# Later ScalarE slots behind VectorE, wider state-space parameter products and shorter recurrence bursts in a two-block float32 kernel

## The chip, the core and the metric

The kernel runs on one core of one Trainium2 chip. The metric is the time of one execution on the device in microseconds, as the median of three. The core's engines run side by side, each through its own queue in order: TensorE (PE, with its weight loads PEld) multiplies, VectorE (DVE) and ScalarE (ACT) work element by element, GpSimd (POOL) and SyncE (SP) issue DMAs here, and ScalarE issues some too. An engine that waits for another holds up all that stands behind it in its queue.

## What is computed

Two transformer blocks on 256 positions (272 in the second) of width 2048, batch 1, in float32. The lines that matter here:

```python
# block 1: token mixing, then a feed-forward with a causal width-3 convolution
p = h @ w_in + b_in                     # u, v, q, k, v_att, z_pool and three gates
merged = (g_sgu * (y_sgu @ w_sgu_out) + g_moba * (y_moba @ w_moba_out)
          + g_pool * (y_pool @ w_pool_out))          # g = sigmoid(gates)
z = h @ w_up
z = w_conv[0] * z2 + w_conv[1] * z1 + w_conv[2] * z + b_conv
gate, val = jnp.split(z, 2, axis=-1)
y = (jax.nn.gelu(gate) * val) @ w_down
...
# block 2: latent attention beside a state-space scan, both gated
y = s5_scan(u, ...)                     # x_t = a * x_(t-1) + B u_t,  y_t = Re(C x_t) + d u_t
y = jax.nn.gelu(y)
ssm_out = (y @ w_glu_val[l]) * jax.nn.sigmoid(y @ w_glu_gate[l])
mixed = jax.nn.sigmoid(g[:, :, 0]) * attn_out + jax.nn.sigmoid(g[:, :, 1]) * ssm_out
h = h + mixed @ w_out[l]
m = rms_norm_2(h, norm_ffn[l])
h = h + (jax.nn.silu(m @ w_ffn_gate[l]) * (m @ w_ffn_up[l])) @ w_ffn_down[l]
```

## The kernel before

**Weights.** Every weight tile of 1 MB is loaded by SyncE (`load_to`) into one of nine `raw` buffers and split into two parts in two half pieces (`split_piece`): ScalarE copies the high part `wh` (L245), VectorE subtracts to get the low part `wl` (L246, in the same nine buffers). Activations are split in the same way. A product is then a pair of matmuls (`mm2`): `wh` against both activation parts at once, 512 columns (L366), and `wl` against the high part, 256 columns (L368). A unit of 16 such pairs fills one of four PSUM tiles `pm`; `join` empties it with a ScalarE copy (L372) and a VectorE addition (L373).

**The order.** It is written out by hand, by generators. The program is a list of units. `run_units` writes a unit's matmuls, and then four *slots*: in each it advances every open evacuation generator by one step (`advance`), oldest first, and then writes one weight half piece for a unit ahead. A `yield` in an evacuation thus means: the next step comes one slot later. After the four slots, one step of the side work (the attention of the block, `pump`) and `bgn` steps of the background work are written: 1.25 a unit for `s5_prep` (the parameters of the state-space scan, during feed-forward 1) and 1 a unit for `s5` (the scan itself, during the input products of block 2 and attention). The modulation rows (`ada`, L547, 128x2048) take the place of a weight piece now and then.

**The stages**, by the profile's time in us: input products of block 1 to 300; gates and the three branches (`block1_in`: `gate`, `branch`) 300 to 640; feed-forward 1 (`ffn1`, four blocks of 22 up-projection units and 12 down-projection units) 690 to 1420; input products of block 2 (`block2_in`) 1500 to 1860, of which the last 32 units are gates (`gfn`); latent attention (`attention2`, with `mla` as side work) from 1860 in units of only four pairs (or triples); state-space gating, output projection (`block2_out`); feed-forward 2 (`ffn2`) 2330 to the end.

**The evacuations that change.** `gate` and `gfn`: join, next slot a tanh on ScalarE (L810, L1416). `branch`: join, product (L834), sum (L838), and for the last branch the activation split (L403, L404). `upfn` in `ffn1`: join, the convolution's first tap on ScalarE (L1234), two taps on VectorE (L1236, L1238), then a Gelu on ScalarE (L1243) for a gate, or a product (L1248) and the activation split (L390, L392) for a value. `ffn2` has the same shape without the convolution.

**The state-space scan.** `s5_prep` works in eight groups. A group multiplies its B by three powers and its C by four powers of the complex decay, one power at a time with six VectorE instructions of 128x128 (`cmul` L1591 to L1596, and L1695 to L1700) and a `yield` behind each power. `s5` runs the recurrence over 66 chunk steps of eight 128x32 instructions on VectorE (L1784 to L1791), with a `yield` after every fourth, and then the output part: per group three reloads `MT` from DRAM (L1801), twelve small matmuls (L1820 to L1822), per two groups a Gelu (L1826), stores `yS` (L1830) and at the end reloads `yD` (L1837) with their splits (L1846, L1847).

Temporaries come from 36 pages of 128x544 (`pg`) and 20 half pages (`hp`).

Of the kernel before, what the change touches and what calls it, by code (L numbers as in the profile page):

```python
# [12 lines left out]
OP = mybir.AluOpType  # L13
# [148 lines left out]
class Kernel:  # L162
    def __init__(self, ctx, tc, ins, out):
        self.tc, self.nc, self.ins, self.out = tc, tc.nc, ins, out
        pool = lambda n, b, **k: ctx.enter_context(tc.tile_pool(name=n, bufs=b, **k))
        self.cp = pool("cp", 1)
        self.wp = pool("wp", 4)
        self.pp = pool("pp", 1)
        self.ps = pool("ps", 4, space=bass.MemoryType.PSUM)
        self.dp = pool("dp", 1, space=bass.MemoryType.DRAM)  # L170
        ctx.enter_context(tc.manual_schedule())
        self.NB = 3
        self.NPG, self.NHP, self.NRAW, self.NW = 36, 20, 9, 4
        self.uid = 0
        self.items, self.raw, self.wt = [], {}, {}
        self.loaded = self.split = self.half = 0
        self.units = []
        self.evq, self.side, self.bg, self.bgn, self.bga = [], [], [], 0, 0.0
        self.sda = 0.0
        self.nstep = 0  # L180
# [76 lines left out]
    def ahead_to(self, last, n):  # L257
# [4 lines left out]
        return last  # L262


    def unit(self, items, fn, ahead=3, pump=1, stages=4, bg=True, flush=False):
# [522 lines left out]
    def block1_in(self):  # L788
# [17 lines left out]
        def gate(store, j, bidx):  # L806
            def fn(p):
                o = self.join(p)
                yield
                nc.scalar.activation(o, o, AF.Tanh, scale=0.5, bias=self.hb[:, bidx:bidx + 1])  # L810
                store[j] = o
            return fn
# [4 lines left out]
        def branch(name, ysrc, n4, tg, place):  # L817
            it = self.add_item(ins[name][n4])
            for jj in range(4):
# [8 lines left out]
                def ev(n, p):  # L828
# [10 lines left out]
                    if place == 2:  # L839
                        yield  # L840
                        xt = self.act_tile()
                        self.split_act(xt, self.mg[n], 0.5)
                        self.X1[n] = xt
# [377 lines left out]
    def ffn1(self):  # L1221
# [5 lines left out]
        def upfn(i):  # L1227
# [3 lines left out]
            def g(p):  # L1231
                z, c = self.join(p), self.hp()[:, :T]
                yield
                nc.scalar.activation(c, z, AF.Identity, scale=self.v("w_conv2", idx), bias=self.v("b_conv", idx))  # L1234
# [6 lines left out]
                if not val:  # L1241
                    yield
                    nc.scalar.activation(c, c, AF.Gelu_apprx_tanh)  # L1243
                    gates[j] = c
                else:
                    while j not in gates:
                        yield
                    nc.vector.tensor_tensor(c, gates.pop(j), c, op=OP.mult)  # L1248
                    yield
                    xt = self.act_tile()  # L1250
# [77 lines left out]
    def block2_in(self):  # L1328
# [83 lines left out]
        def gfn(j):  # L1412
            def g(p):
                o = self.join(p)
                yield
                nc.scalar.activation(o, o, AF.Tanh, scale=0.5)  # L1416
                yield
                nc.scalar.dma_start(self.gd[:, j], o)
            return g
# [178 lines left out]
    def s5_prep(self):  # L1598
# [7 lines left out]
        lr, li, ls = (sv[:, i * 32:(i + 1) * 32] for i in range(3))  # L1606
        w = [wk[:, i * 32:(i + 1) * 32] for i in range(17)]
        yield
# [23 lines left out]
        tt(apr[:, 0], mag, cs, op=OP.mult)  # L1632
        tt(api[:, 0], mag, sn, op=OP.mult)
        tmp = (w[7], w[8])
        for l in range(1, 4):
# [22 lines left out]
        tt(ci, ci, den, op=OP.mult)  # L1658
        yield

        def bc(x):
            return x[:, :, None].to_broadcast([128, 4, 32])

        def v4(x):
# [5 lines left out]
        for g in range(8):  # L1670
# [7 lines left out]
            sc = self.pg(n="s5c")  # L1678
            u1, u2, B0, B1 = (v4(sc[:, i * 128:(i + 1) * 128]) for i in range(4))
            nci = v4(self.hp(n="s5n")[:, :128])  # L1680
            self.cmul(B0, B1, br, bi, bc(cr[:, tl]), bc(ci[:, tl]), (u1, u2))
            ts(nci, c_i, -1.0, None, op0=OP.mult)
# [3 lines left out]
            yield  # L1686
            for j in range(3):
                pr, pi = bc(apr[:, 2 - j, tl]), bc(api[:, 2 - j, tl])
                self.cmul(BA[0][:, :, j], BA[1][:, :, j], B0, B1, pr, pi, (u1, u2))
                yield  # L1690
            yield
            CA = [v44(self.pg(n="CA")) for _ in range(2)]
            for l in range(4):
                pr, pi = bc(apr[:, l, tl]), bc(api[:, l, tl])
                tt(u1, c_r, pr, op=OP.mult)  # L1695
                tt(u2, c_i, pi, op=OP.mult)
                tt(CA[0][:, :, l], u1, u2, op=OP.subtract)
                tt(u1, nci, pr, op=OP.mult)
                tt(u2, c_r, pi, op=OP.mult)
                tt(CA[1][:, :, l], u1, u2, op=OP.subtract)  # L1700
                yield

# [29 lines left out]
    def s5(self):  # L1732
# [49 lines left out]
        for c in range(1, 67):  # L1782
# [8 lines left out]
            tt(ci, ci, tm[3], op=OP.add)  # L1791
            if c % 4 == 3:
                yield
# [58 lines left out]
    def block2_out(self):  # L1852
# [10 lines left out]
        for i in range(8):  # L1863
            ig = self.add_item(ins["w_gg"][i])
            iv = self.add_item(ins["w_gv"][i])
            for it, kind in ((ig, 0), (iv, 1)):
                for jj in range(2):
# [10 lines left out]
                    def ev(n, p, kind):  # L1878
                        if kind == 0:
                            o = self.join(p)  # L1880
                            yield
                            nc.scalar.activation(o, o, AF.Tanh, scale=0.5)
# [101 lines left out]
    def ffn2(self):  # L1984
# [4 lines left out]
        def upfn(i):  # L1989
            j, val = divmod(i, 2)  # L1990

            def g(p):
                v = self.join(p)
                yield
                if not val:
                    nc.scalar.activation(v, v, AF.Silu)
                    gates[j] = v
                else:
# [4 lines left out]
                    v = None  # L2003
                    yield
                    xt = self.act_tile()
# [67 lines left out]
```

## Time and profile before

| | |
|---|---|
| median of 3 runs | 3058.28 us (3053.97 to 3065.57) |
| the profiled execution's own time | 3066.25 us |
| its span, first to last instruction | 3064.5 us |
| TensorE busy | 2935.0 us (96%) |
| VectorE busy | 2136.2 us (70%) |
| ScalarE busy | 1477.6 us (48%) |
| GpSimd busy | 56.9 us (2%), 109 instructions |
| mean granted TensorE clock | 0.981 |

A row of the profile names the line of the kernel, the engine, what is written and read, and a duration. L366 is line 366. Idle time stands in brackets or behind a bar, with the work that ended it. "PEclk" is the granted share of TensorE's full clock; 0.50 is the lower of its two levels.

### The profile page before, as it was taken

To read this page: it belongs to the slowest core of one execution; us is meant where nothing else is said; L and a number is where in the kernel's file an instruction comes from. 1 tells how busy PE (TensorE), PEld (TensorE's weight loads), DVE (VectorE), ACT (ScalarE), POOL (GpSimd) and SP (SyncE) were. 2 spreads that over 40 slices of the span, in tenths; PEclk is the share of its full clock that TensorE was granted. 3 is DMA by queue.
4 is the path that set the end of the run, shared out by engine and by line. 5 is a ranking of instruction groups with operands and counts; after the bars stand their busy time and mean duration, and the time that the engine had idled before them with its cause. 6 is when DMAs were issued, how large, how long until landed. Compare 5 with 4: busy or idle time off the path is not lost.

```text
span 3064.5 us, 41672 instructions
## 1 busy us (share of the span) xinstructions
PE 2935.0 (96%) x16204; PEld 2508.0 (82%) x16204; DVE 2136.2 (70%) x3789; ACT 1477.6 (48%) x2443; POOL 56.9 (2%) x109
## 2 busy tenths in 40 slices
PE   6999989889999999999899899999999999999998
PEld 4998878778788787887799787778888888888887
DVE  7889989877878888777546956656655545555555
ACT  5445445456554545455444344445445434444343
POOL 0000000000000000000000000000000000000000
PEclk9999999999999999999899998999999999999999
DMA  9977768774466676655465574235664555555554
GB/s 363 351 290 276 265 249 342 263 275 161 162 233 244 210 270 235 217 192 189 153 227 185 176 256 156 98 133 208 222 217 164 178 196 191 189 187 187 193 188 129
DMA packets 127224, 660.39 MB, mean 215 GB/s; under 512 B 23009, under 2 KB 36065, under 8 KB 57393
## 3 DMA queue, kind: packets, MB, share of 16 engines
q1 hardware_dynamic: 86258, 603.30, 54.6%
q10 hardware_dynamic: 34464, 35.47, 3.7%
q0 software_dynamic: 6304, 18.95, 1.7%
q8 instruction: 128, 2.10, 0.3%
q14 instruction: 70, 0.57, 0.1%
HBM read 632.42 MB, written 25.23 MB: 215 GB/s over the span
## 4 chain that ended last, share of the span: by engine, by line
PE 65%; DVE 22%; ACT 9%; issue 3%; DMA 1%; ACTq 0%; SPq 0%; DVEq 0%
PE pm L366 19%; PE pm L368 10%; DVE wl L246 7%; PE pm L384 7%; PE pm L386 7%; PE pm L385 7%; ACT wh L245 5%; DVE raw L547 3%; PE pm L352 3%; PE pm L353 3%; PE pm L354 3%; DVE hp L1238 1%; DVE hp L373 1%; DVE hp L1236 1%; ACT hp L1234 1%
## 5 line engine op out<-in xcount | busy, mean ns | idle before, releaser
L366 PE MATMUL pm<-act,wh 128*128 128x512 f32 x4704 | 1674.8, 399 | 28.5 <-DVE hp L373 18.7
L246 DVE TENSOR_TENSOR wl<-raw,wh 128x1024 fp32r<-128x1024 f32 (+1 forms) x972 | 1144.4, 1197 | 302.6 <-ACT wh L245 289.1
L368 PE MATMUL pm<-act,wl 128*128 128x256 f32 x4704 | 1328.3, 282 | 24.2 <-DVE wl L246 24.1
L366 PEld LDWEIGHTS pm<-act,wh 128*128 128x128 f32 x4704 | 890.3, 189 | 243.5 <-DVE hp L373 23.0
L245 ACT ACTIVATE wh<-raw 128x1024 fp32r<-128x1024 f32 (+1 forms) x972 | 968.8, 1030 | 242.5 <-PE pm L385 114.4
L368 PEld LDWEIGHTS pm<-act,wl 128*128 128x128 f32 x4704 | 892.7, 190 | 35.3 <-DVE wl L246 33.8
L384 PE MATMUL pm<-wh,act 128*128 128x512 f32 (+1 forms) x1072 | 430.4, 401 | 15.3 <-ACT act L738 6.1
L386 PE MATMUL pm<-wl,act 128*128 128x512 f32 (+1 forms) x1072 | 425.9, 397 | 0.7 <-DVE wl L246 0.7
L385 PE MATMUL pm<-wh,act 128*128 128x512 f32 (+1 forms) x1072 | 424.9, 396 | 0.5 <-DVE act L740 0.5
L373 DVE TENSOR_TENSOR hp<-hp,pm 128x256 f32<-128x256 f32 x336 | 140.1, 417 | 301.3 <-ACT hp L372 301.2
L372 ACT ACTIVATE hp<-pm 128x256 f32<-128x256 f32 x336 | 125.5, 377 | 425.4 <-PE pm L368 406.0
L384 PEld LDWEIGHTS pm<-wh,act 128*128 128x128 f32 (+1 forms) x1072 | 202.4, 189 | 68.3 <-ACT wh L245 7.2
L386 PEld LDWEIGHTS pm<-wl,act 128*128 128x128 f32 (+1 forms) x1072 | 202.3, 189 | 51.8 <-DVE wl L246 3.5
L385 PEld LDWEIGHTS pm<-wh,act 128*128 128x128 f32 (+1 forms) x1072 | 202.8, 189 | 50.3 <-DVE act L740 1.5
L352 PE MATMUL pm<-act,wh 128*128 128x256 f32 (+1 forms) x768 | 224.0, 292 | 8.4 <-DVE qk L373 8.2
L354 PE MATMUL pm<-act,wl 128*128 128x256 f32 (+1 forms) x768 | 221.5, 288 | 1.3 <-DVE wl L246 1.3
L353 PE MATMUL pm<-act,wh 128*128 128x256 f32 (+1 forms) x768 | 222.0, 289 | 0.3 <-DVE act L740 0.3
L547 DVE SCALAR_TENSOR_TENSOR raw<-raw,cond 128x2048 f32<-128x2048 f32 x96 | 219.0, 2285 | 4.5 <-DMA raw<-w_ada 4.4
L352 PEld LDWEIGHTS pm<-act,wh 128*128 128x128 f32 x768 | 148.3, 193 | 10.7 <-DVE qk L373 9.3
L353 PEld LDWEIGHTS pm<-act,wh 128*128 128x128 f32 x768 | 148.6, 193 | 0.8 <-DVE act L740 0.7
L354 PEld LDWEIGHTS pm<-act,wl 128*128 128x128 f32 x768 | 147.5, 192 | 1.7 <-DVE wl L246 1.7
L390 ACT ACTIVATE act<-hp 128x256 fp32r<-128x256 f32 x88 | 36.8, 418 | 138.3 <-DVE hp L1248 107.4
(329 smaller groups left out, 1771.1 us busy)
## 6 DMA issues: line engine op xcount, KB each, us to landing
raw<-w_ada SPq DMA_DIRECT2D x96, 1024.0 KB, 6.1
raw<-w_up SPq DMA_DIRECT2D x88, 1024.0 KB, 4.8
raw<-w_ff SPq DMA_DIRECT2D x88, 1024.0 KB, 4.8
raw<-w_in SPq DMA_DIRECT2D x81, 1024.0 KB, 5.0
raw<-w_st SPq DMA_DIRECT2D x37, 1024.0 KB, 6.3
raw<-w_out SPq DMA_DIRECT2D x32, 1024.0 KB, 5.7
raw<-w_down SPq DMA_DIRECT2D x32, 1024.0 KB, 5.1
raw<-w_fd SPq DMA_DIRECT2D x32, 1024.0 KB, 4.9
```

Source lines behind the costliest of these rows:

```text
L245: nc.scalar.activation(vh[:, ks], r[:, ks], AF.Copy)
L246: nc.vector.tensor_tensor(vl[:, ks], r[:, ks], vh[:, ks], op=OP.subtract)
L352: nc.tensor.matmul(o, wh[:, kw, c], x[:, 0, sl], start=start, stop=False, skip_group_check=True)
L353: nc.tensor.matmul(o, wh[:, kw, c], x[:, 1, sl], start=False, stop=False, skip_group_check=True)
L354: nc.tensor.matmul(o, wl[:, kw, c], x[:, 0, sl], start=False, stop=stop, skip_group_check=True)
L366: nc.tensor.matmul(p.rearrange("p (a t) -> p a t", a=2), wh[:, kw, c], x, start=start, stop=False, skip_group_check=True)
L368: nc.tensor.matmul(p[:, T:], wl[:, kw, c], x[:, 0], start=False, stop=stop, skip_group_check=True)
L373: self.nc.vector.tensor_tensor(o, o, p[:, :T], op=OP.add)
L384: nc.tensor.matmul(o, x[:, 0, tok], wh[:, kw], start=start, stop=False, skip_group_check=True)
L385: nc.tensor.matmul(o, x[:, 1, tok], wh[:, kw], start=False, stop=False, skip_group_check=True)
L386: nc.tensor.matmul(o, x[:, 0, tok], wl[:, kw], start=False, stop=stop, skip_group_check=True)
L547: self.nc.vector.scalar_tensor_tensor(o, o, 0.5, self.cond, op0=OP.mult, op1=OP.mult, accum_out=self.m(seg, n))
```

## The change

`later(n)` is a generator of n empty steps. Where an evacuation had one `yield` between a VectorE step and a ScalarE step that needs it, there are now two or three. The parameters of the state-space scan are multiplied for all three powers of B, or all four of C, in one instruction of 128x384 or 128x512, with repeated operands; a group goes from 18 steps of background work to 14, and the reversed powers are copied once in front. The recurrence yields after every second chunk step. The software DMA's scratch shrinks from the default to 4096 bytes of a partition, and the space goes to two more pages and seven more half pages. Computed values are the same.

```diff
@@ -170,7 +170,7 @@
-        self.NPG, self.NHP, self.NRAW, self.NW = 36, 20, 9, 4
+        self.NPG, self.NHP, self.NRAW, self.NW = 38, 27, 9, 4
@@ -261,6 +261,12 @@
+    @staticmethod
+    def later(n):
+
+        for _ in range(n):
+            yield
...
@@ -806,7 +812,7 @@
                 o = self.join(p)
-                yield
+                yield from self.later(3)
                 nc.scalar.activation(o, o, AF.Tanh, scale=0.5, bias=self.hb[:, bidx:bidx + 1])
@@ -837,7 +843,7 @@
                     if place == 2:
-                        yield
+                        yield from self.later(2)
                         xt = self.act_tile()
@@ -1230,7 +1236,7 @@
                 z, c = self.join(p), self.hp()[:, :T]
-                yield
+                yield from self.later(2)
                 nc.scalar.activation(c, z, AF.Identity, scale=self.v("w_conv2", idx), bias=self.v("b_conv", idx))
@@ -1239,14 +1245,14 @@
                 if not val:
-                    yield
+                    yield from self.later(2)
                     nc.scalar.activation(c, c, AF.Gelu_apprx_tanh)
...
                     nc.vector.tensor_tensor(c, gates.pop(j), c, op=OP.mult)
-                    yield
+                    yield from self.later(2)
                     xt = self.act_tile()
@@ -1412,7 +1418,7 @@
                 o = self.join(p)
-                yield
+                yield from self.later(3)
                 nc.scalar.activation(o, o, AF.Tanh, scale=0.5)
...
@@ -1657,9 +1665,19 @@
+        for j in range(3):
+            nc.vector.tensor_copy(rev[:, 0, j], apr[:, 2 - j])
+            nc.vector.tensor_copy(rev[:, 1, j], api[:, 2 - j])
+        yield
...
+        def bc4(x):
+            return x[:, :, :, None].to_broadcast([128, x.shape[1], 4, 32])
+
+        def rp(x, n):
+            return x[:, None].to_broadcast([128, n, 4, 32])
@@ -1676,29 +1694,41 @@
...
-            for j in range(3):
-                pr, pi = bc(apr[:, 2 - j, tl]), bc(api[:, 2 - j, tl])
-                self.cmul(BA[0][:, :, j], BA[1][:, :, j], B0, B1, pr, pi, (u1, u2))
-                yield
...
+            u1, u2 = wide(t1, 3), wide(t2, 3)
+            o0, o1 = (BA[i].rearrange("p t j c -> p j t c")[:, :3] for i in range(2))
+            pr, pi = bc4(rev[:, 0, :, tl]), bc4(rev[:, 1, :, tl])
+            tt(u1, rp(B0, 3), pr, op=OP.mult)
+            tt(u2, rp(B1, 3), pi, op=OP.mult)
+            tt(o0, u1, u2, op=OP.subtract)
+            yield
+            tt(u1, rp(B0, 3), pi, op=OP.mult)
+            tt(u2, rp(B1, 3), pr, op=OP.mult)
+            tt(o1, u1, u2, op=OP.add)
+            yield
...
-            for l in range(4):
-                pr, pi = bc(apr[:, l, tl]), bc(api[:, l, tl])
-                tt(u1, c_r, pr, op=OP.mult)
-                tt(u2, c_i, pi, op=OP.mult)
-                tt(CA[0][:, :, l], u1, u2, op=OP.subtract)
-                tt(u1, nci, pr, op=OP.mult)
-                tt(u2, c_r, pi, op=OP.mult)
-                tt(CA[1][:, :, l], u1, u2, op=OP.subtract)
-                yield
+            u1, u2 = wide(t1, 4), wide(t2, 4)
+            o0, o1 = (CA[i].rearrange("p t l c -> p l t c") for i in range(2))
+            pr, pi = bc4(apr[:, :, tl]), bc4(api[:, :, tl])
+            tt(u1, rp(c_r, 4), pr, op=OP.mult)
+            tt(u2, rp(c_i, 4), pi, op=OP.mult)
+            tt(o0, u1, u2, op=OP.subtract)
+            yield
...
@@ -1789,7 +1819,7 @@
             tt(ci, ci, tm[3], op=OP.add)
-            if c % 4 == 3:
+            if c % 2:
                 yield
@@ -1878,7 +1908,7 @@
                             o = self.join(p)
-                            yield
+                            yield from self.later(2)
                             nc.scalar.activation(o, o, AF.Tanh, scale=0.5)
@@ -1991,7 +2021,7 @@
                 v = self.join(p)
-                yield
+                yield from self.later(2 if not val else 1)
...
@@ -2001,7 +2031,7 @@
                     v = None
-                    yield
+                    yield from self.later(2)
                     xt = self.act_tile()
@@ -2060,7 +2090,7 @@
-    nc = bacc.Bacc("TRN2", target_bir_lowering=False, num_devices=1)
+    nc = bacc.Bacc("TRN2", target_bir_lowering=False, num_devices=1, dynamic_dma_scratch_size=4096)
```

In feed-forward 1, ScalarE's queue between two joins. Before:

```order
L372 ACTIVATE hp_8558<-pm_8525 128x256
L245 ACTIVATE wh_8564<-raw_8437 128x1024
L1234 ACTIVATE hp_8561<-hp_8558,vecs 128x256
L245 ACTIVATE wh_8564<-raw_8437 128x1024
L390 ACTIVATE act_8574<-hp_8561 128x256
L372 ACTIVATE hp_8616<-pm_8582 128x256
```

After, at the same kind of place (line numbers are the changed kernel's: L378 is the join, L1240 the convolution's tap, L1249 the Gelu, L396 the split):

```order
L378 ACTIVATE hp_8539<-pm_8506 128x256
L245 ACTIVATE wh_8545<-raw_8434 128x1024
L1249 ACTIVATE hp_8487<-hp_8487 128x256
L245 ACTIVATE wh_8545<-raw_8434 128x1024
L1240 ACTIVATE hp_8542<-hp_8539,vecs 128x256
L1755 ACTIVATE BT_8557<-pd_8329 128x512
L1755 ACTIVATE BT_8560<-pd_8330 128x512
L378 ACTIVATE hp_8596<-pm_8563 128x256
L396 ACTIVATE act_8603<-hp_8542 128x256
```

The tap on the tile just joined has moved behind both weight copies, and the Gelu or the split has moved into the next unit, behind that unit's join.

In the gate stage of block 1, ScalarE's queue for one gate unit. Before:

```order
L372 ACTIVATE hp_3184<-pm_3151 128x256
L810 ACTIVATE hp_3184<-hp_3184,hb 128x256
L245 ACTIVATE wh_3193<-raw_3077 128x1024 x2
L400 ACTIVATE act_3199<-hp_3136 128x256
L950 ACTIVATE hp_3204<-pd_3202,vecs 128x256
```

After:

```order
L378 ACTIVATE hp_3184<-pm_3151 128x256
L245 ACTIVATE wh_3192<-raw_3077 128x1024 x2
L816 ACTIVATE hp_3184<-hp_3184,hb 128x256
L406 ACTIVATE act_3199<-hp_3136 128x256
L956 ACTIVATE hp_3204<-pd_3202,vecs 128x256
```

The tanh (L810, now L816) stands behind the two weight copies. The rows of the pooling branch behind it stay.

At the start of attention, ScalarE's queue up to the first exponentials (L1546, now L1552). Before:

```order
L1483 ACTIVATE qk_17081<-pm_17068 128x272
L1483 ACTIVATE qk_17096<-pm_17083 128x272
L1483 ACTIVATE qk_17111<-pm_17098 128x272
L1511 ACTIVATE vv_17126<-pm_17113 16x512
L245 ACTIVATE wh_17130<-raw_16929 128x1024 x2
L1546 ACT_TABLE_LOAD
L1546 ACTIVATE sm_17141,sm_17143<-sm_17141,sm_17143 128x144
```

After:

```order
L1831 DMA MT_16732<-s5d 128x512
L1489 ACTIVATE qk_16761<-pm_16748 128x272
L1856 ACTIVATE yt_16701<-yt_16701 128x512
L1517 ACTIVATE vv_16778<-pm_16765 16x512
L245 ACTIVATE wh_16782<-raw_16535 128x1024 x2
L1552 ACT_TABLE_LOAD
L1552 ACTIVATE sm_16793,sm_16795<-sm_16793,sm_16795 128x144
L1552 ACTIVATE sm_16793,sm_16795<-sm_16793,sm_16795 128x272
L1860 DMA yS<-yt_16701 32x8x64 x4
L1517 ACTIVATE vv_16818<-pm_16805 128x512
L1831 DMA MT_16828<-s5d 128x512
```

The scan's output part (reloads MT L1831, Gelu L1856, stores yS L1860), which ended before the first exponentials, now stands among them; Gelu and exponential use different tables, so a table load stands at each change between them.

## Rows read from the trace of the kernel before

**Rows 1.** Busy line of the page: us, share, instructions

```profile
PE 2935.0 (96%) x16204; PEld 2508.0 (82%) x16204; DVE 2136.2 (70%) x3789; ACT 1477.6 (48%) x2443; POOL 56.9 (2%) x109
```

**Rows 2.** Stretches: length, PE, PEld, DVE, ACT, POOL busy, PEclk, DMA share, GB/s

```profile
300.00:640.00 340.00, 314.97 (x1642) 261.85 (x1641) 300.56 (x475) 161.54 (x291) 0.00 (x0) 0.97 0.75 284
...
690.00:1390.00 700.00, 681.07 (x3633) 577.65 (x3632) 561.26 (x1075) 373.87 (x622) 33.85 (x63) 0.99 0.60 213
...
1700.00:1766.00 66.00, 55.90 (x306) 46.49 (x305) 63.06 (x323) 24.61 (x38) 0.00 (x0) 1.00 0.51 171
...
1860.00:1990.00 130.00, 120.72 (x600) 90.55 (x599) 83.73 (x179) 59.08 (x129) 4.32 (x8) 0.93 0.34 116
```

**Rows 3.** TensorE's longest wait in each stretch: total us, times, longest

```profile
PE pm L366 <- DVE hp L373: 18.7, 10, 4.8
...
PE pm L368 <- DVE wl L246: 14.0, 14, 2.1
...
PE pm L368 <- DVE wl L246: 10.1, 10, 1.1
...
PE pm L352 <- DVE qk L373: 8.2, 4, 3.5
```

**Rows 4.** Busy time and clock in three short stretches, columns as in rows 2

```profile
967.00:970.20 3.20, 2.92 (x9) 2.53 (x10) 2.86 (x6) 1.97 (x4) 0.00 (x0) 0.50 0.97 364
...
1772.60:1779.30 6.70, 6.70 (x27) 6.21 (x28) 5.22 (x6) 3.55 (x6) 0.00 (x0) 0.50 0.89 312
...
1875.00:1885.00 10.00, 7.56 (x32) 6.96 (x32) 9.68 (x23) 5.32 (x10) 0.00 (x0) 0.50 0.15 48
```

**Rows 5.** Timeline in feed-forward 1: start, duration, [idle before]

```profile
953.35 1.23 DVE L246 TENSOR_TENSOR wl<-raw,wh 128x1024 fp32r<-128x1024 f32 x1 [0.48 <-ACT wh L245]
...
951.77 0.60 ACT L1234 ACTIVATE hp<-hp,vecs 128x256 f32<-128x256 f32 x1 [0.85 <-DVE hp L373]
```

**Rows 6.** VectorE's longest wait from 690 to 1390: total us, times, longest

```profile
DVE wl L246 <- ACT wh L245: 60.4, 112, 4.2
```

**Rows 7.** Timeline of TensorE without waits: first matmuls of two pairs

```profile
2504.36 0.39 PE L366 MATMUL pm<-act,wh 128*128 128x512 f32 x1
...
2504.71 0.40 PE L366 MATMUL pm<-act,wh 128*128 128x512 f32 x1
```

**Rows 8.** VectorE's timeline: first, second of a parameter burst, next work

```profile
955.41 0.28 DVE L1591 TENSOR_TENSOR s5c<-s5c,s5p 128x128 f32<-128x128 f32 x1
955.61 0.28 DVE L1592 TENSOR_TENSOR s5c<-s5c,s5p 128x128 f32<-128x128 f32 x1
...
956.99 0.41 DVE L373 TENSOR_TENSOR hp<-hp,pm 128x256 f32<-128x256 f32 x1
```

**Rows 9.** VectorE groups by form: busy us, mean ns of one, idle before

```profile
L246 DVE TENSOR_TENSOR wl<-raw,wh 128x512 fp32r<-128x512 f32 x12 | 8.2, 684 | 0.1
...
L1695 DVE TENSOR_TENSOR s5c<-s5m,s5p 128x128 f32<-128x128 f32 x28 | 8.0, 286 | 0.1
```

**Rows 10.** VectorE's waits from 300 to 600: total us, times, longest

```profile
DVE hp L373 <- ACT hp L372: 14.5, 12, 1.4
...
DVE wl L246 <- ACT wh L245: 2.9, 7, 0.5
```

**Rows 11.** VectorE's timeline in the recurrence: join, first small one, next join

```profile
1728.02 0.41 DVE L373 TENSOR_TENSOR hp<-hp,pm 128x256 f32<-128x256 f32 x1
...
1731.00 0.20 DVE L1784 TENSOR_TENSOR tm<-X,a 128x32 f32<-128x32 f32 x1
...
1734.97 0.41 DVE L373 TENSOR_TENSOR hp<-hp,pm 128x256 f32<-128x256 f32 x1
```

**Rows 12.** Reloads MT, ns min/median/max, us to landing; a table load

```profile
L1801 ACTq DMA_DIRECT2D MT<-s5d x24: 387/454/1280, 1764.1 to 1842.2; - x24
...
DMA to landing us min/median/max: 2.8/4.5/9.5
...
L1546 ACT ACT_TABLE_LOAD x1 | 1.3, 1283 | 0.0
```

More of the change, by code (lines that the diff above doesn't have):

```diff
@@ L1606, in s5_prep @@
         lr, li, ls = (sv[:, i * 32:(i + 1) * 32] for i in range(3))
-        w = [wk[:, i * 32:(i + 1) * 32] for i in range(17)]
+        w = [wk[:, i * 32:(i + 1) * 32] for i in range(11)]
+        w += [par[:, 256 + i * 32:288 + i * 32] for i in range(2)]
         yield
@@ L1633, in s5_prep @@
         tt(api[:, 0], mag, sn, op=OP.mult)
+        rev = wk[:, 352:544].rearrange("p (a j t) -> p a j t", a=2, j=3)
         tmp = (w[7], w[8])
@@ L1678, in s5_prep @@
             sc = self.pg(n="s5c")
-            u1, u2, B0, B1 = (v4(sc[:, i * 128:(i + 1) * 128]) for i in range(4))
-            nci = v4(self.hp(n="s5n")[:, :128])
-            self.cmul(B0, B1, br, bi, bc(cr[:, tl]), bc(ci[:, tl]), (u1, u2))
+            B0, B1, nci, v1 = (v4(sc[:, i * 128:(i + 1) * 128]) for i in range(4))
+            t1, t2 = self.pg(n="s5u"), self.pg(n="s5u")
+            v2 = v4(t1[:, :128])
+            self.cmul(B0, B1, br, bi, bc(cr[:, tl]), bc(ci[:, tl]), (v1, v2))
             ts(nci, c_i, -1.0, None, op0=OP.mult)
@@ L1686, in s5_prep, with wide @@
             yield
-            for j in range(3):
-                pr, pi = bc(apr[:, 2 - j, tl]), bc(api[:, 2 - j, tl])
-                self.cmul(BA[0][:, :, j], BA[1][:, :, j], B0, B1, pr, pi, (u1, u2))
-                yield
+            def wide(x, n):
+                return x[:, :n * 128].rearrange("p (j t c) -> p j t c", j=n, t=4)
+            u1, u2 = wide(t1, 3), wide(t2, 3)
[8 more added lines that the diff above has]
+            tt(o1, u1, u2, op=OP.add)
             yield
             CA = [v44(self.pg(n="CA")) for _ in range(2)]
-            for l in range(4):
-                pr, pi = bc(apr[:, l, tl]), bc(api[:, l, tl])
-                tt(u1, c_r, pr, op=OP.mult)
-                tt(u2, c_i, pi, op=OP.mult)
-                tt(CA[0][:, :, l], u1, u2, op=OP.subtract)
-                tt(u1, nci, pr, op=OP.mult)
-                tt(u2, c_r, pi, op=OP.mult)
-                tt(CA[1][:, :, l], u1, u2, op=OP.subtract)
-                yield
+            u1, u2 = wide(t1, 4), wide(t2, 4)
[5 more added lines that the diff above has]
+            yield
+            tt(u1, rp(nci, 4), pr, op=OP.mult)
+            tt(u2, rp(c_r, 4), pi, op=OP.mult)
+            tt(o1, u1, u2, op=OP.subtract)
+            yield
             pk = self.pss()
```

## The prediction, made before the changed kernel was run

> **What bounds the kernel now.** I read the page's busy line first: TensorE is busy 96% of the span [rows 1]. The matmul stream is not changed, so the change can only take time from the rest: 3064.5 - 2935.0 = 129.5 us in which TensorE stands idle, and the stretches in which its clock is granted at half. Second, the busy time by stretch says where the idle time lies [rows 2]: the gate stage (300 to 640) loses 340 - 315.0 = 25.0, the first feed-forward stage (690 to 1390) 18.9, the recurrence (1700 to 1766) 10.1, the attention stage (1860 to 1990) 9.3, together 63 us. The other 66 lie mostly in the start, the stage boundaries and the tail, which the diff leaves alone. Third, TensorE's own waits name who ends them [rows 3]: in all four a VectorE row, joins (L373) in the gates and in attention, low weight halves (L246) in the other two. VectorE is busy 300.6 of 340 us in the gates and 63.1 of 66 in the recurrence [rows 2], so there it is the limit itself; in the feed-forward it has 561 of 700 and is late in bursts. Fourth, the clock: in the few us at and behind the larger waits the rows show 0.50, that is 1.2 GHz instead of 2.4, after TensorE had idled [rows 4].
>
> **The change part by part.** *Later ScalarE steps, feed-forward 1.* VectorE ends a join, starts a weight piece, and then idles 0.48 us before the second piece [rows 5]: ScalarE's second weight copy stands behind the convolution step L1234, which had itself waited 0.85 us for that join. Such waits of a weight piece for ScalarE's copy make 60.4 us in 112 times in this stretch [rows 6]. With the step two slots later both copies stand ahead of it, so where VectorE is late it no longer idles. Over the 22 up-projection units of one of the four blocks that is 22 x 0.48 = 10.6 us of VectorE time; TensorE's idle time of a block is 18.9 / 4 = 4.7 us on average, less than half of it. What is late next is a burst of VectorE: TensorE's unit is 16 pairs of matmuls at 0.35 us [rows 7], 5.6 us, and a unit with a modulation row and two state-space pieces can still pass that.
>
> *State-space parameters at once.* Six narrow instructions take from 955.41 to 956.99, 1.58 us; the first two start 0.20 apart, so with three such gaps the three dependent ones take 0.33 each [rows 8]. Seven such bursts a group are replaced (three for B, four for C): 11.1 us. The wide forms have no row. The nearest are 128 elements at 286 ns and 512 at 684 ns [rows 9], 1.04 ns an element, so 384 cost about 0.55 us (an estimate from these rows). With the narrow ones' overlap (a start 0.08 before the end where independent, 0.04 after it where dependent) half of B is 0.47 + 0.59 + 0.59 = 1.65 us, half of C 0.60 + 0.72 + 0.72 = 2.05, together 7.4 us a group. That saves 3.7 us x 8 = 30 us of VectorE. It does not all help: a group now takes 14 slots instead of 18, so the work per slot hardly falls; the saving is that it ends before the last of the four blocks is through. One slot's burst grows from 1.6 to 2.05 us. Bounds: if the broadcast or strided forms ran at half speed, a group would cost 14 us, nothing is saved and the bursts double; at full overlap it is the 30 us.
>
> Sum for this stage: of the 18.9 us I take 14 as gone, and with them most of the three half-clock stretches, of which one of 3.2 us is shown [rows 4] and the others have 3.3 each; they cost half of that, 4.9 us, and I take 4. So -18, between 0 and -23.
>
> [...]
>
> *Gate stage.* Here VectorE is the limit, so only its idle time can be won. Between 300 and 600 it idles 14.5 us behind joins and 2.9 for weight copies [rows 10]. The second kind goes when the tanh moves behind the copies. The joins wait behind the softmax's exponentials, which do not move. The split moved in the three-branch merge becomes the first thing of the next unit, where it stands in front of the same join as before: no change. So -3, between 0 and -9.
>
> *Recurrence in half bursts.* A period is 6.95 us from join to join, of which 32 small instructions take 1731.00 to 1734.97, 3.97 [rows 11]. TensorE's unit is 5.6 us, and it waits 10.1 us in ten times [rows 3]. With two steps a slot VectorE needs 6.95 - 1.99 = 4.96 us, below 5.6, so the wait goes. The same steps now last 33 slots instead of 17, each with no more work than that. I take -10, between -5 and -13 (with half of the 6.7 us at half clock behind it [rows 4]).
>
> *What the recurrence pushes away.* Its 16 extra slots move the output part of the state-space scan (24 reloads MT, 96 matmuls, four Gelu, 16 stores yS) from units of 5.6 us into attention units of four pairs, 1.4 us, on ScalarE between the joins and the exponentials. MT lands 4.5 us after its issue in the median [rows 12]; a group now has some four short units and its neighbour's matmuls for that, about 7 us, less what ScalarE's queue is late. I take 1 us of wait for seven of the groups, +7. Against it: the 8.2 us of waits for joins [rows 3] stand where four rotations and eight splits L1847 share VectorE; the splits leave them, -3. So +4. Low bound -9, if these waits and half their low clock go; high bound +22, if all added ScalarE work shows: 24 issues of MT and 12 of yS at 0.45 each, four table loads at 1.28 [rows 12].
>
> A Gelu between exponentials changes the table: four loads more here, one fewer in the feed-forward. A load takes 1.28 us [rows 12]. The Trainium skill, "ScalarE: Activation LUTs", section "What ACT_TABLE_LOAD costs", adds about as much again for a drain, 2.66 us a switch, and speaks against mixing. No row here shows that drain; by the page the high bound would be 5.5 us higher.
>
> *More buffers.* Of the added seven half and two full pages no row shows a wait that they end; they carry the longer lives of joined tiles, 0. The smaller scratch belongs to GpSimd's few DMA issues: 0, between 0 and +5. The other moved steps (state-space gating, the last feed-forward) lie outside the four stretches: 0.
>
> **Sum.** -18 - 3 - 10 + 4 = -27 us. The profiled execution took 3066.25 (its span 3064.5), 8 us above the median of 3058.28; 3066.25 - 27 = 3039, and put on the median 3031.
>
> **The rivals.** *The waits come back* (no change): the wide bursts and the moved tail make VectorE or ScalarE late at other places. For it: VectorE is at 88% in the gate stage, and one slot's burst grows. Then -10 for the recurrence, +8 in attention, -5 elsewhere: -7, 3051. *All goes*: every bound at its low end, -23 - 9 - 13 - 9 = -54, 3004; against it stands VectorE's load in the gates. *Slower*: ScalarE becomes the limit at the start of attention. Price: its 22 us exposed and 10 us of waits for MT, +32; with -10 from the recurrence and nothing else won that is +22, 3080. It decides from the point where ScalarE's work of a unit exceeds TensorE's; today it is busy 59 of 130 us there [rows 2], and 22 more make 62%, so the point is reached only locally. *The steps do not move*: the order on ScalarE excludes it; it would leave the recurrence, the wide forms and the tail, about 3050.
>
> **How the numbers follow.** A measurement tells this kernel from no change at about 0.5%, 15 us. Forecast (3016 to 3043) 0.57, all goes (below 3016) 0.14, waits come back (3043 to 3073) 0.22, slower 0.07. Faster by over 0.5% is 0.57 + 0.14 = 0.71, same 0.22, slower 0.07. The range of 8 in 10 leaves out about 0.07 below 3005 and 0.13 above 3057.
>
> **What would show it.** Right: no TensorE wait in the recurrence; VectorE's idle time behind weight copies in the feed-forward far below 60 us and TensorE's there under 5; fewer stretches of clock 0.50. Wrong: waits for MT or joins of more than 15 us at the start of attention, or wide instructions well over 0.7 us.

## The result and the profile after

The changed kernel takes 3015.37 us in the median (3011.45 to 3020.89), the kernel before 3060.3 beside it: a ratio of 0.9855, 95% interval 0.983 to 0.9881, or 45 us less. Timed a second time it was 3012.65 us, 0.9849 (0.9834 to 0.9864). The forecast was 3031 with a range of 3005 to 3057: right in sign and inside the range, but 16 us short. Most of what follows is about those 16 us, and about smaller terms that were wrong and cancelled in part.

The busy line and the chain's shares on the page of the changed kernel, to set beside [rows 1]:

```profile
PE 2912.4 (97%) x16204; PEld 2502.8 (83%) x16204; DVE 2099.0 (70%) x3555; ACT 1475.7 (49%) x2446; POOL 56.9 (2%) x109
...
PE 77%; DVE 3%; ACT 1%; DMA 0%; issue 0%; ACTq 0%; DVEq 0%
```

The same chain in the page of the kernel before:

```profile
PE 65%; DVE 22%; ACT 9%; issue 3%; DMA 1%; ACTq 0%; SPq 0%; DVEq 0%
```

The chain that ends last ran through VectorE and ScalarE for 31% of the span before, and for 4% after. TensorE's instructions are as many as before.

To see where the time went, I cut every kernel's span at the same matmuls of the program. Two of the pieces matter: feed-forward 1 up to the next stage (the first row of each pair), and the recurrence with the first part of attention, where all of the scan's output lies (the second row, "scan stage" below). Busy time by stretch, columns as in [rows 2], of the kernel before:

```profile
706.62:1489.93 783.31, 760.79 (x3978) 641.56 (x3977) 620.25 (x1180) 418.65 (x703) 38.10 (x71) 0.99 0.61 215
1649.47:2027.53 378.06, 357.53 (x1968) 292.58 (x1966) 259.35 (x861) 163.20 (x309) 6.48 (x12) 0.97 0.48 166
```

and of the changed kernel:

```profile
702.57:1446.53 743.96, 743.96 (x3979) 638.41 (x3977) 588.84 (x946) 414.10 (x701) 38.13 (x71) 1.00 0.63 227
1603.47:1974.10 370.63, 355.46 (x1967) 292.40 (x1966) 259.19 (x861) 167.86 (x313) 6.48 (x12) 0.97 0.49 169
```

Feed-forward 1 is 39.4 us shorter, the scan stage 7.4. What lies ahead of them gives 4.1, between them 2.6, behind them 1.5: together the 55 us between the two spans. (These two profiled executions lie 6 us above and 4 us below the medians of 3060.3 and 3015.37, hence 55 and not 45.)

In feed-forward 1 TensorE is busy 743.96 of 743.96 us at full clock: no wait is left. The waits of VectorE (702 to 1390, the first row) and of ScalarE (700 to 1390) in the changed kernel show what took their place; columns are total us, times, longest:

```profile
DVE wl L246 <- ACT wh L245: 55.5, 54, 8.9
```

```profile
ACT hp L378 <- PE pm L374: 110.3, 50, 8.0
...
ACT act L396 <- DVE hp L1254: 24.1, 17, 3.1
...
ACT hp L1249 <- DVE hp L1244: 23.0, 16, 2.7
...
ACT hp L1240 <- DVE hp L379: 17.9, 17, 2.9
```

and ScalarE's of the kernel before in the same 700 to 1390:

```profile
ACT act L390 <- DVE hp L1248: 97.6, 39, 2.7
ACT hp L1243 <- DVE hp L1238: 78.0, 36, 2.3
ACT hp L1234 <- DVE hp L373: 35.8, 41, 3.3
ACT hp L372 <- PE pm L368: 25.8, 6, 7.9
```

With its split, Gelu and tap ScalarE waited 211.4 us for VectorE before and waits 65.0 us now; its longest wait is now for TensorE, the engine that should be last. VectorE's idle time behind weight copies [rows 6] is hardly smaller in sum, 55.5 us for 60.4, but it is half as many waits, and they are those of an engine that is ahead. The prediction named that sum as a sign and expected it "far below 60 us"; the sum was no sign, TensorE's waits were.

### The profile page after: what moved, and what is told of

Same layout as the page of the kernel before. It is cut to its first block, busy times and chain, and to the rows that moved or that the text cites. A ratio compares the mean times of both kernels' runs of the same rounds, so it can differ in the third digit from the quotient of the medians.

```text
span 3009.6 us, 41394 instructions
## 1 busy us (share of the span) xinstructions
PE 2912.4 (97%) x16204; PEld 2502.8 (83%) x16204; DVE 2099.0 (70%) x3555; ACT 1475.7 (49%) x2446; POOL 56.9 (2%) x109
## 4 chain that ended last, share of the span: by engine, by line
PE 77%; DVE 3%; ACT 1%; DMA 0%; issue 0%; ACTq 0%; DVEq 0%
PE pm L372 30%; PE pm L374 16%; PE pm L390 7%; PE pm L392 7%; PE pm L391 7%; PE pm L358 1%; DVE wl L246 1%; PE pm L360 1%; PE pm L359 1%; PE pd L502 1%; PE pd L1538 0%; PE pd L1800 0%; ACT jk L485 0%; PE pd L1736 0%; PE pd L1537 0%
## 5 line engine op out<-in xcount | busy, mean ns | idle before, releaser
L372 PEld LDWEIGHTS pm<-act,wh 128*128 128x128 f32 x4704 | 887.7, 189 | 239.5 <-DVE hp L379 20.5
L378 ACT ACTIVATE hp<-pm 128x256 f32<-128x256 f32 x336 | 126.9, 381 | 558.7 <-PE pm L374 557.9
L379 DVE TENSOR_TENSOR hp<-hp,pm 128x256 f32<-128x256 f32 x336 | 140.2, 418 | 279.4 <-ACT hp L378 279.1
L2043 DVE TENSOR_TENSOR x<-pm,x 128x512 f32<-128x512 f32 x32 | 22.1, 692 | 90.9 <-PE pm L392 90.8
```

What stands on the lines that cost most here:

```text
L372: nc.tensor.matmul(p.rearrange("p (a t) -> p a t", a=2), wh[:, kw, c], x, start=start, stop=False, skip_group_check=True)
L379: self.nc.vector.tensor_tensor(o, o, p[:, :T], op=OP.add)
```

## The experiments

All the ratios are to the kernel before, timed beside it. The two stage columns are lengths in us from one profiled execution of each, cut as above.

| kernel | median us | ratio (95% interval) | feed-forward 1 | scan stage |
|---|---|---|---|---|
| before | 3057 to 3060 | 1 | 783.3 | 378.1 |
| the change | 3015.37 | 0.9855 (0.983 to 0.9881) | 744.0 | 370.6 |
| pools | 3055.78 | 0.9995 (0.9984 to 1.0007) | 782.6 | 376.6 |
| pools_conv | 3023.44 | 0.9891 (0.9871 to 0.991) | 743.9 | 369.6 |
| pools_tap | 3037.28 | 0.993 (0.9918 to 0.9943) | 763.9 | 371.1 |
| pools_gelu | 3046.77 | 0.9961 (0.9948 to 0.9974) | 766.9 | 374.6 |
| pools_wide | 3052.18 | 0.9975 (0.9961 to 0.9989) | 775.7 | 378.1 |
| pools_burst | 3060.65 | 1.0002 (0.9989 to 1.0015) | 781.7 | 378.3 |
| after_again | 3012.65 | 0.9849 (0.9834 to 0.9864) | 744.0 | 367.3 |
| no_wide | 3017.36 | 0.9866 (0.9849 to 0.9883) | 743.9 | 379.4 |
| no_burst | 3009.18 | 0.984 (0.9824 to 0.9856) | 744.0 | 362.8 |
| burst32 | 3003.21 | 0.9818 (0.9804 to 0.9833) | 744.0 | 354.6 |
| burst3 | 3005.74 | 0.9824 (0.9807 to 0.984) | 744.0 | 362.8 |
| burst3_split | 2996.46 | 0.9791 (0.9776 to 0.9806) | 740.6 | 362.2 |

### One part of the change at a time

**pools**: the buffers and the scratch alone.

```diff
-        self.NPG, self.NHP, self.NRAW, self.NW = 36, 20, 9, 4
+        self.NPG, self.NHP, self.NRAW, self.NW = 38, 27, 9, 4
-    nc = bacc.Bacc("TRN2", target_bir_lowering=False, num_devices=1)
+    nc = bacc.Bacc("TRN2", target_bir_lowering=False, num_devices=1, dynamic_dma_scratch_size=4096)
```

> The kernel before with nothing but the larger page pools (38 and 27) and the software DMA scratch of 4096 bytes; every order of instructions stays. Theory: buffers and scratch bear nothing of the gain; 0 us against before, between -4 and +4, and the same stretches of waits (feed-forward 1 about 19 us of TensorE idle time, recurrence ten waits of 1.1 us). Rival: buffers were short in feed-forward 1 and in attention; then 10 us or more of the 45 show here already.

0.9995: nothing, as the prediction said. The next five kernels have these pools too.

**pools_conv**: the three later slots of feed-forward 1.

```diff
                 z, c = self.join(p), self.hp()[:, :T]
-                yield
+                yield from self.later(2)
                 nc.scalar.activation(c, z, AF.Identity, ...)
...
-                    yield
+                    yield from self.later(2)
                     nc.scalar.activation(c, c, AF.Gelu_apprx_tanh)
...
-                    yield
+                    yield from self.later(2)
                     xt = self.act_tile()
```

> The larger pools and the later ScalarE slots of feed-forward 1 alone (the three of the convolution's evacuation); narrow products of the state-space parameters, long recurrence bursts. Theory A, the order on ScalarE makes the waits: most of the 40 us that feed-forward 1 lost go here, -30 us against before (-22 to -38), TensorE's idle time there below 4 us. Theory B, VectorE's load in bursts makes them: -10 us (0 to -16), over 10 us of idle time left in feed-forward 1.

**pools_wide**: the products of the state-space parameters in wide instructions, as in the diff of the change.

```diff
-            for j in range(3):
-                pr, pi = bc(apr[:, 2 - j, tl]), bc(api[:, 2 - j, tl])
-                self.cmul(BA[0][:, :, j], BA[1][:, :, j], B0, B1, pr, pi, (u1, u2))
-                yield
+            tt(u1, rp(B0, 3), pr, op=OP.mult)
...
```

> The larger pools and the wide products of the state-space parameters alone; ScalarE's steps stand in their old slots. Theory A (the order on ScalarE makes the waits): -8 us against before (0 to -15), at least 10 us of TensorE idle time left in feed-forward 1. Theory B (VectorE's load makes them): -30 us (-22 to -38), idle time there below 4 us.

Feed-forward 1 by stretch, of pools and then of pools_conv:

```profile
701.69:1484.29 782.60, 758.42 (x3978) 640.35 (x3977) 620.51 (x1180) 418.61 (x702) 38.27 (x71) 0.99 0.61 215
704.92:1448.82 743.90, 743.90 (x3979) 638.45 (x3977) 613.77 (x1180) 415.00 (x701) 38.09 (x71) 1.00 0.63 227
```

and of pools_wide:

```profile
705.88:1481.59 775.71, 758.40 (x3979) 642.49 (x3977) 594.05 (x946) 417.86 (x702) 38.09 (x71) 0.99 0.61 217
```

The slots alone bring the stage to the length that it has in the whole change, with VectorE doing the same 1180 instructions (613.77 us busy, 620.51 in pools). Taking 26 us of load off VectorE (594.05) gives only 6.9 us of the stage and leaves 17.3 idle. By the medians the two are 35 and 6 us faster than the kernel before, both within Theory A. It holds: the order on ScalarE made the waits, and VectorE's load counted only while that order stood.

**pools_tap** and **pools_gelu** split the three slots: the tap alone, and the Gelu and the split alone (the first, and the other two, pieces of the diff of pools_conv).

> The larger pools and, of the three later slots of feed-forward 1, only the convolution's first tap; Gelu and split stay where they were. Theory A1, from the prediction (the tap that waits for the join holds up the second weight copy): most of the 33 us, -22 against before (-16 to -30). Theory A2 (ScalarE's larger waits are those of the Gelu and the split for VectorE, 78 and 98 us, which hold up the next join and copies): -8 (0 to -14).

> The larger pools and only the Gelu's and the split's later slots; the tap stays in front of the second weight copy. Theory A1 (the tap): -8 us against before (0 to -14). Theory A2 (Gelu and split): -22 (-16 to -30).

By the ratios 21 and 12 us, together the 33 of pools_conv. So the tap is the larger cause, as the prediction had it, but the Gelu and the split count for more than A1 allowed in the stage itself: 18.7 us for the tap, 15.7 for the others. The stage's rows of pools_tap, then of pools_gelu:

```profile
706.76:1470.61 763.85, 750.36 (x3979) 639.29 (x3978) 614.27 (x1180) 412.67 (x702) 38.30 (x71) 1.00 0.62 221
```

```profile
707.85:1474.73 766.88, 752.09 (x3978) 639.22 (x3977) 617.65 (x1180) 415.95 (x702) 38.29 (x71) 1.00 0.62 220
```

Each leaves 13 to 15 us of idle time. Each of the three steps waited in ScalarE's queue for something that VectorE was late with, and so held up the copies that VectorE needed next. How the second share divides between Gelu and split is not shown: they were moved together.

**pools_burst**: the recurrence in bursts of two.

```diff
-            if c % 4 == 3:
+            if c % 2:
                 yield
```

> The larger pools and the recurrence in bursts of two steps alone. My theory: the ten waits of 1.1 us go with the half-clock stretch behind them (-13 us), and the output part that is pushed into attention gives 6 back: -7 us against before (-3 to -12). Rival 1, the tail gives all back: 0 or slower. Rival 2, the tail is hidden: -13 us.

1.0002: rival 1. The first part of the recurrence was shorter by 8.8 us, as foreseen; the stage as a whole was 1.8 longer than in pools. The scan stage's row of pools, then of pools_burst:

```profile
1643.72:2020.27 376.55, 355.62 (x1967) 291.72 (x1966) 259.31 (x861) 163.26 (x309) 6.50 (x12) 0.97 0.48 167
```

```profile
1644.45:2022.76 378.31, 365.22 (x1967) 299.16 (x1966) 261.87 (x861) 168.03 (x313) 6.47 (x12) 0.94 0.48 166
```

What took the gain back is the clock, not idle time: TensorE idles 13.1 us here for 20.9 in pools, but the granted clock is 0.94 for 0.97. The clock has two levels, so that the time at the lower one is twice the missing share of the stretch: 2 x 0.06 x 378 = 45 us here for 23 in pools. This is not one execution alone: the mean clock of the whole program is 0.979 over the 11 timed executions of pools_burst and 0.983 over the 12 of pools.

### Parts taken out of the change, and other bursts

**no_wide**: the wide products undone (pools_wide's diff the other way).

> The changed kernel with the state-space parameters in narrow instructions, one power at a time. Theory, from the run with the later slots of feed-forward 1 alone (no TensorE wait left there, stage as long as in the changed kernel): the wide products are worth nothing once the slots have moved, so this is as the changed kernel within 3 us. Rival: they are worth what they are worth alone, 8 us, so this is 8 us slower than the changed kernel.

Feed-forward 1 is 743.9 us long, the same: the wide products are worth nothing once the slots have moved. On the medians no_wide is 4.7 us above after_again, with overlapping intervals, so that they alone decide neither for the theory (within 3 us) nor for the rival (8 us). What differs most between their profiles is the scan stage, where both have the same instructions in the same order. Its row of no_wide, then of after_again:

```profile
1603.00:1982.43 379.43, 367.57 (x1968) 301.72 (x1967) 259.18 (x861) 167.67 (x313) 6.49 (x12) 0.93 0.48 165
```

```profile
1605.18:1972.53 367.35, 355.24 (x1968) 290.55 (x1966) 259.27 (x861) 167.81 (x313) 6.49 (x12) 0.97 0.50 171
```

TensorE idles 11.9 and 12.1 us, but the clock is 0.93 in one and 0.97 in the other. That is 2 x 0.07 x 379 = 53 us at 1.2 GHz against 22; the clock is shown to two places, so that each may be off by 4 us. Some 31 us more at the lower level made the stage 12.1 us longer, about 0.4 us for each. So one profiled execution of this stage is uncertain by about 12 us.

**no_burst**: the change with the long bursts of before.

```diff
-            if c % 2:
+            if c % 4 == 3:
                 yield
```

> The changed kernel with the long recurrence bursts of before (a step aside after every fourth chunk). Theory A, from the stage lengths of the run with the bursts alone (recurrence -8.8 us, attention +10.5): the finer bursts are worth nothing on the median; 3015 us (3010 to 3020), as the changed kernel, with ten waits of 1.1 us back in the recurrence and fewer at the start of attention. Rival, from the stage lengths of the changed kernel (-8.8 and +2.8): they are worth 6 us there, so 3021 here (3017 to 3026).

**burst32**, **burst3**: bursts of three and two in turn (27 slots), and of three (22).

```diff
-            if c % 2:
+            if c % 5 in (0, 3):
                 yield
```

```diff
-            if c % 2:
+            if c % 3 == 0:
                 yield
```

> The changed kernel with recurrence bursts of three and two chunk steps in turn, 27 slots instead of 33 (and 17 before). VectorE then needs 6.95 - 1.5 = 5.5 us a unit on average against TensorE's 5.6, so the recurrence stays without long waits, and the output part ends some six units earlier. If the collision of the output part with the softmax is what eats the gain: attention 4 us shorter, 3011 us (3006 to 3015). If what eats it is ScalarE's and VectorE's added work wherever it stands: 3015, as the changed kernel.

> The changed kernel with a step aside after every third chunk step of the recurrence: 22 slots instead of 33. With the gates' tanh moved, four steps a unit gave a period of 6.58 us, so three give 6.58 - 1.0 = 5.58, just TensorE's 5.59. Theory, the collision in attention is what made the finer bursts cost more than they gave: no waits in the recurrence and the output part ahead of the exponentials, 3001 us (2997 to 3005), 12 less than the changed kernel. Rival: VectorE is too tight at three steps and waits of 0.3 to 0.5 us a unit come, 3007.

The scan stage's rows of no_burst, then of burst32:

```profile
1602.89:1965.71 362.82, 348.01 (x1967) 285.37 (x1966) 256.53 (x861) 164.13 (x309) 6.47 (x12) 0.99 0.50 173
```

```profile
1605.82:1960.44 354.62, 346.19 (x1967) 285.47 (x1966) 257.95 (x861) 165.09 (x311) 6.50 (x12) 1.00 0.51 177
```

Without the finer bursts the stage is 362.8 us, shorter than the 370.6 and 367.3 of the change with them. By the medians no_burst and the changed kernel can't be told apart (0.984 against 0.9855 and 0.9849), and by the paragraph on no_wide a few us of one profiled execution prove little; but here as in pools and pools_burst the finer bursts come out at zero or above, and nothing speaks for the 6 us that were forecast. no_burst lies 1 us below the range of its Theory A, and the rival (3021) is out. TensorE idles as long with the finer bursts as without (15.2 and 12.1 us for 14.8); again it is the clock that is lower with them, 0.97 for 0.99 in the stage, and over whole executions 0.984 in the mean of eight for 0.987 in the mean of four. burst32, timed beside no_burst, is 6 us faster (3002.39 to 3004.96 against 3007.45 to 3014.55): no wait in the recurrence, 8.4 us idle in the stage, almost no time at the lower clock. That is 8 us below the 3011 of the collision theory and below its range, and further from the rival's 3015; how much of it is the collision and how much the clock is not shown. burst3 came 5 us above its forecast: no wait in the recurrence, but one of 8.2 us for the softmax in attention.

**burst3_split**: burst3, and the split of the three-branch merge one slot later still.

```diff
                     if place == 2:
-                        yield from self.later(2)
+                        yield from self.later(3)
                         xt = self.act_tile()
                         self.split_act(xt, self.mg[n], 0.5)
```

> The same and, in the three-branch merge, the split three slots later instead of two, which puts ScalarE's split behind the next join, where two left it in front. Theory, VectorE idles 0.48 us in each of those short units for that split and TensorE waits there (4.16 and 3.76 us, 560 to 580): 3 us less than the kernel with bursts of three (0 to -6). Rival, VectorE's own work bounds these units: 0.

The gate stage (the pieces of the program between the same two matmuls) by stretch, of burst3:

```profile
277.25:601.65 324.40, 301.59 (x1652) 253.19 (x1651) 294.02 (x467) 157.66 (x290) 0.00 (x0) 0.97 0.74 280
```

and of burst3_split:

```profile
276.94:595.28 318.34, 301.09 (x1652) 253.25 (x1651) 292.87 (x467) 158.06 (x290) 0.00 (x0) 0.97 0.76 285
```

6.1 us less, twice the forecast, 5.6 of it idle time. (The medians differ by 9.3; the other 3.4 are in feed-forward 1, which is 740.6 us long here, and are not explained.) VectorE's timeline in three short units of burst3_split shows why, with the join L379 in front of the split L410:

```profile
566.27 0.41 DVE L379 TENSOR_TENSOR hp<-hp,pm 128x256 f32<-128x256 f32 x1
...
567.97 0.41 DVE L379 TENSOR_TENSOR hp<-hp,pm 128x256 f32<-128x256 f32 x1
568.54 0.42 DVE L410 SCALAR_TENSOR_TENSOR act<-pt,act 128x256 fp32r<-128x256 f32 x1
...
569.67 0.41 DVE L379 TENSOR_TENSOR hp<-hp,pm 128x256 f32<-128x256 f32 x1
```

A unit takes 1.70 us from join to join; with the split in front it was 2.16 (565.46, 567.62, 569.78 in burst32's timeline), of which 0.48 is VectorE's wait for ScalarE's half of the split:

```profile
567.27 0.43 DVE L410 SCALAR_TENSOR_TENSOR act<-pt,act 128x256 fp32r<-128x256 f32 x1 [0.48 <-ACT act L409]
567.62 0.41 DVE L379 TENSOR_TENSOR hp<-hp,pm 128x256 f32<-128x256 f32 x1
```

This kernel, at 2996.46 us, beats both the kernel before and the changed one (by 16 us beside after_again). burst32 with this split was not tried.

## Why the prediction was right, and where it was not

**Feed-forward 1: right cause, the term mis-sized** (-18, at most -23, for a measured -39.4). The working names the tap alone as what held up the second weight copy; pools_gelu shows that the Gelu and the split, which it does not price, were worth 15.7 us of the stage by themselves. In the sum, four things were left out. First, all of the idle time went, not 14 of 18.9. Second, I cut the stage at 1390; it goes on to 1490, and the whole of it had 783.31 - 760.79 = 22.5 us idle. Third, the time at the lower clock was 17 us with the 6.8 behind a wait at 1441, not 10; at 0.4 each that is 7. These make 29.5. Fourth, the idle column understates a wait. TensorE's timeline of the kernel before, at the longest wait of the stage's first block:

```profile
791.01 0.40 PE L366 MATMUL pm<-act,wh 128*128 128x512 f32 x1
793.47 0.39 PE L368 MATMUL pm<-act,wl 128*128 128x256 f32 x1 [2.06 <-DVE wl L246]
793.69 0.39 PE L366 MATMUL pm<-act,wh 128*128 128x512 f32 x1
793.92 0.28 PE L368 MATMUL pm<-act,wl 128*128 128x256 f32 x1
```

From one L366 to the next it took 2.68 us, where 0.35 is a pair without waits [rows 7]: 2.33 lost, 2.06 shown. With the 23 waits of the stage that is about 6 more, an estimate from this one. The rest, some 4 us, is not accounted for; stalls too short to appear as idle are possible, which no run here shows.

**The state-space parameters: price right, worth wrong.** The wide instructions took what was worked out, 0.55 and 0.68 us; VectorE's groups by form in the changed kernel:

```profile
L1714 DVE TENSOR_TENSOR BA<-s5u,s5u 128x384 f32<-128x384 f32 x8 | 4.5, 558 | 0.3
...
L1724 DVE TENSOR_TENSOR s5u<-s5m,s5p 128x512 f32<-128x512 f32 x8 | 5.5, 685 | 0.1
```

But the prediction let them share the stage's gain, and named VectorE's bursts as what would be late next. Nothing was late next. pools_conv and no_wide agree on zero; alone they give 6.9 us of the stage.

**Gates: -3 for about -1.** The gate stage by stretch, of pools and then of the changed kernel:

```profile
273.33:598.72 325.39, 302.28 (x1653) 254.22 (x1652) 294.64 (x467) 159.29 (x290) 0.00 (x0) 0.97 0.73 277
```

```profile
275.06:599.57 324.51, 301.88 (x1653) 253.23 (x1651) 294.00 (x467) 157.69 (x290) 0.00 (x0) 0.97 0.75 279
```

TensorE idles 22.6 us there in the changed kernel and 23.1 in pools; over all the profiles it is 22.6 to 25.0 with the old tanh and 21.8 to 22.8 with the moved one, burst3_split aside. VectorE's waits for copies did shrink (2.9 [rows 10] to 0.9), but TensorE did not wait for those. "No change" for the split was right, for the reason given: with two slots it is still in front of the join. burst3_split shows what one more was worth.

**The tanh of block 2's gates: left out.** The prediction counted the recurrence's units with their old period of 6.95 us, though the change moves the tanh (L1416) of those very units. In no_burst, with the long bursts, TensorE's timeline has the waits at

```profile
1672.54 0.38 PE L374 MATMUL pm<-act,wl 128*128 128x256 f32 x1 [0.71 <-DVE wl L246]
1679.11 0.39 PE L374 MATMUL pm<-act,wl 128*128 128x256 f32 x1 [0.72 <-DVE wl L246]
```

a period of 6.57, and the scan stage is 6.8 us shorter than in pools_conv, which has the old tanh and otherwise the same steps there (362.8, 369.6; the clock is 0.99 in both). The row of pools_conv, to set beside that of no_burst above:

```profile
1606.31:1975.89 369.58, 350.64 (x1968) 287.16 (x1966) 259.19 (x861) 162.93 (x309) 6.48 (x12) 0.99 0.49 170
```

**Recurrence and tail: -10 + 4 for a sum near zero or above.** The first term held: the first part of the recurrence took 98.86 us before and takes 90.06, with no wait. The second was mis-sized, and its reason was wrong. Seven waits for a reload MT were to make 7 us; none of TensorE's idle time in the changed kernel stands against one (they landed 3.6 us after the issue in the median; one weight load waited 0.4 us, and burst32 has three such waits of 2.2 us together). The largest of the waits that came are the softmax's, whose steps now share ScalarE's and VectorE's queues with the scan's output. TensorE's waits in the changed kernel from 1771.9 to 1884, and the longest one behind that, which is also one for the softmax:

```profile
PE pm L372 <- DVE qk L379: 3.4, 2, 2.9
PE pd L1567 <- DVE sm L1560: 2.0, 1, 2.0
...
PE pd L1537 <- DVE yt L1855: 1.1, 1, 1.1
...
1889.74 0.48 PE L1580 MATMUL pd<-pmt,vv 16*128 16x256 f32 x1 [4.21 <-DVE pmt L1572]
```

The last splits of the scan's output stand between two softmax rows and hold ScalarE and VectorE for over 2 us each; a softmax row, a join and two weight pieces stand behind them on VectorE before that copy L1572. ScalarE's and VectorE's timeline:

```profile
1880.34 2.29 ACT L1876 ACTIVATE act<-yD 128x256 fp32r<-128x256 f32 x4
...
1881.15 2.18 DVE L1877 TENSOR_TENSOR act<-yD,act 128x256 fp32r<-128x256 f32 x4
```

The four added table loads are there too. ScalarE's timeline around one, between the softmax and a Gelu:

```profile
1838.25 0.18 ACT L1552 ACTIVATION_READ_ACCUMULATOR sm<-sm,sm 128x1 f32 x1
1838.45 1.28 ACT L1856 ACT_TABLE_LOAD   x1
1839.74 0.63 ACT L1856 ACTIVATE yt<-yt 128x512 f32<-128x512 f32 x1
```

From the end of the operation ahead to the start of the one behind, the switch took 1.31 us. The drain that the Trainium skill, "ScalarE: Activation LUTs", section "What ACT_TABLE_LOAD costs", adds to it (2.66 us in all) does not show; the trace disagrees.

In sum these waits took little: behind the first part of the recurrence TensorE idles 15.2 us in the stage, for 13.7 in the kernel before (20.5 less the 6.9 of the first part). What the finer bursts cost is mostly the clock behind such waits. Behind the wait of 2.9 us (its end is at 1783.49) it falls; busy time by stretch of the changed kernel:

```profile
1784.60:1794.80 10.20, 9.39 (x41) 8.71 (x39) 9.95 (x32) 0.77 (x2) 0.00 (x0) 0.50 0.49 161
```

From no_burst to the change the stage has 0.4 us more idle time at most and 15 us more at the lower level (22 for 7). The prediction counted low-clock stretches only as something to be won and had no term for new ones. Which of the waits brings the clock down for how long is not shown; no_wide and after_again differ in it with the same instructions.

So the -6 that the prediction took from the bursts came from the tanh instead: pools to pools_burst +1.8 us, no_burst to the change +4.5 to +7.8 in the stage. That the scan stage came out at -7.4 us, close to the -6, is luck.

**The rivals.** "All goes" (3004) is nearest: it was right for feed-forward 1 and wrong for the rest. "The waits come back" holds for the bursts alone. ScalarE as the limit of attention did not come: in about the same stretch of the program it was busy 69.98 of 161.3 us after (1775.4 to 1936.7, scan's output included), 43%, and 59.08 of 130 before [rows 2], 45%.

**The signs.** No TensorE wait in the recurrence, and none in feed-forward 1, came true. So did the absence of the others: joins made TensorE wait 5.7 us in the scan stage and not over 15, and the wide instructions stayed under 0.7 us. The granted clock of the whole program rose from 0.981 to 0.985. VectorE's idle time behind the copies was the wrong sign.

## What to carry to other kernels

A step that waits for another engine belongs in its queue behind whatever that other engine needs next: look in the waits for an engine off the critical path that waits on the engine it feeds, and move that step, before making anything faster. Sum a stage by its whole length, and price a wait from start to start with the slow clock behind it. When steps are cut finer, ask what now ends later and what stands there, and read the granted clock beside the idle time: bursts of two ended the recurrence's waits and lost the gain to the lower clock, three and two steps in turn kept it.

## What was not expected of the hardware

The same instructions in the same order, with nearly the same idle time (12.1 and 11.9 us), took 367.35 and 379.43 us, with a granted clock of 0.97 and 0.93. And a wait that is shown as 2.06 us idle cost 2.33. In the rows at 791 to 794 the matmul ahead is shown for 0.40, while L368 starts 0.23 behind its L366 where nothing waits (793.69, 793.92): that hides 0.17. The other 0.10 is that the first L368 behind the wait took 0.22 to the next start and not 0.12, the rest of a pair of 0.35.
